# Keys' stacks behind the naturals, gates that begin without GpSimd taps, and rotation tables behind weight halves, in a two-block transformer kernel

## The chip, the cores and the metric

The kernel runs on one core of a Trainium2 chip. The metric is the time of one execution on the device in microseconds (us), given as the median of several runs. The engines are called as the profile calls them: PE is TensorE, ACT is ScalarE, DVE is VectorE, POOL is GpSimd, and SP is SyncE, whose queue issues all the loads here. Line numbers (L113) are those of the kernel before; behind the edits the changed kernel's lines stand up to six lines further down (L113 becomes L114, L488 becomes L489, L521 becomes L524, L908 becomes L914).

## The reference

One sequence of S = 512 tokens and width D = 1024, in float32, passes two blocks. Cut to what matters:

```python
# block 1
h = rms_norm(x, norm1_g)
q, k_c, v_c, k_s, v_s, k_w, v_w, g_nsa, u_conv, g_merge = split(h @ w_in)
# 8 query heads in 2 groups; compressed keys (a 2-layer MLP over windows of 32
# tokens), selected keys and windowed keys; three softmaxes, gated by g_nsa
y_attn = nsa_attention(q, k_c, v_c, k_s, v_s, k_w, v_w, g_nsa, ...) @ w_attn_br
a, gate = split(u_conv)
z = causal_dwconv(a * sigmoid(gate), conv_dw_w) + conv_dw_b      # 31 taps, 512 channels
y_conv = silu(layer_norm(z)) @ w_conv_br
g_a, g_b = split(sigmoid(g_merge))
x = x + (g_a * y_attn + g_b * y_conv) @ w_out
u = causal_dwconv(rms_norm(x) @ ffn_w_up, ffn_dw_w) + ffn_dw_b   # 3 taps
x = rms_norm(x + (silu(u1) * u2) @ ffn_w_down, final_g)
# block 2: two layers, each with a modulation (shift, scale, gate) from c
h = rms_norm(x) * (1 + scale) + shift
x = x + gate * even_mixer(h)   # grouped attention with axial rotations, and a latent attention
x = x + gate * odd_mixer(...)  # windowed attention with a sink per head
return rms_norm(x)
```

The rotation of the even mixer multiplies normalised queries and keys (with a learned gain per head dimension) by cosines and sines. The products of gain and cosine or sine don't depend on the data that flows through the network; they are the "tables" of this change.

## The kernel before

**Products in three parts.** Each float32 weight is split into a high half, rounded for PE, and a low half, the rest. `wload` (L102) does this for a tile of 128 x 512: SP loads the raw tile into a buffer, ACT copies it rounded (L112), and POOL or DVE subtracts (L113). `wpools` says in turn which buffers the next tiles use and which engine subtracts: raw tiles lie in `t` (6 buffers) or `wr` (3), halves in `wh` and `wl` (4 each). A raw buffer is free for the next load when its subtraction is done. `mm3` (L123) makes three products per tile of K, and the first of a group (L133) uses the low half, so that PE waits for the subtraction, and the releaser of such a wait reads "wl L113". A PSUM bank of the pools `pg` and `ps` takes each result and is freed by the evictions that read it.

**Order of the work.** The code is traced top to bottom; then a scheduler lays each engine's instructions out in an order of its own, in which an instruction may overtake others that were traced before it. Two things bind it here: inside `in_order(...)` the named engines keep the traced order, and inside `issue_after(x)` an instruction follows instruction x. Each engine then carries its instructions out strictly in the order laid out; one that waits holds up all that stands behind it on its engine. The same holds for the loads in SP's queue.

**Keys and naturals (L467 to L493).** The two key tiles `tkb` of the selected and the windowed branch are each stacked twice by `stack_k` (L294): two ACT copies (L297, L299) and two DVE operations for each stack, so eight ACT copies in all. Then four "naturals", products with tokens in the partitions, give the values: each is evicted by ACT with a scale (L488), then stacked by `stack_v` (ACT at L305 and DVE), and its gate columns get a tanh (L492). The naturals' PSUM banks are the wide ones, `ps` and `pg` in turn; behind them on PE come the query products and the compression of keys (L425 to L439), whose weights ACT copies at L430, whose sum ACT copies at L436 and PE transposes at L439.

**Merge gates and taps (L685 to L722).** The depthwise convolution's taps are worked beside the sixteen merge gates (`merge_gate(m, b)`, each 24 products with two weight tiles, both subtracted on POOL). Channels 1 to 3 have their taps on DVE, paced by n0 and n1. Channel 0 has its taps on POOL: `conv_tap(0, t)` is a scaled copy on ACT (L520) and an addition on POOL (L521). Those still to be done at this point are in `first`; there are 16 of them, and `gates(0, 7, ...)` spreads them evenly over its 14 gates:

```python
            for t in rest[len(rest) * i // len(todo):len(rest) * (i + 1) // len(todo)]:
                conv_tap(0, t)
```

POOL keeps the traced order here. Ahead of the gates, POOL works at the scores' normalisation (L614) and at the fourth convolution channel's input (L508, L509).

**Down projection and tables (L805 to L911).** The down projection has 22 tiles of K. Tiles 0 to 10 are taken early, tiles 11 to 17 in the loop at L823 over eight column blocks m, whose weight tiles (two per block, one of 128 x 512 and one of 128 x 384) are subtracted on POOL, and tiles 18 to 21 in `by_halves` (L830), first for tokens 0 to 255, then for the rest, so that the normalisation of the first half runs beside the second. The weights of tiles 18 to 21 (`halves_weights`, one tile for each m) stay in the pools `m` and `h`, since both halves use them; they are subtracted on DVE and POOL in turn, and POOL's last, for m = 7, is named `h` in the trace. All of it is independent data, and the scheduler mixes the weight tiles of L823 and of `by_halves`. The four rotation tables are traced behind (L902 to L910), as multiplications on POOL:

```python
            G.tensor_tensor(t, cc(tname).rearrange("p (i d) -> p i d", d=64),
                            row[:, go:go + 64].unsqueeze(1).to_broadcast([128, 4, 64]), op=OP.mult)
```

They need only constants, so the scheduler puts them far ahead of their trace, among the subtractions of L823.

Of the kernel before, what the change touches and what calls it, by code (L numbers as in the profile page):

```python
# [14 lines left out]
OP = mybir.AluOpType  # L15
# [28 lines left out]
def build(ctx, tc, I, out):  # L44
    nc = tc.nc
    PE, A, V, G = nc.tensor, nc.scalar, nc.vector, nc.gpsimd
# [16 lines left out]
    def new(p, shape=(128, 512), dt=F32, tag=None):  # L63
        count[0] += 1
        return pools[p].tile(list(shape), dt, tag=tag or p, name=f"{p}{count[0]}")

    def f(ap):
        return ap.bitcast(F32)
# [4 lines left out]
    row = new("k", (128, 144), tag="row")  # L73
# [4 lines left out]
    def cv(name, i=0, n=1):  # L78
        o = VEC[name][0] + i
        return vec[:, o:o + n]  # L80

    def cc(name, i=0, n=None):
        for t, d in zip(cst, CST):
            if name in d:
                o, m = d[name]
                return t[:, o + i:o + i + (m if n is None else n)]
# [11 lines left out]

    wpools = [[("t", "wh", "wl", G), ("t", "wh", "wl", V), ("wr", "wh", "wl", G)]]
    wcount = [0]  # L100

    def wload(src, kt, n, p=None):  # L102
        wcount[0] += 1
        pr, ph, pl, eng = wpools[0][wcount[0] % len(wpools[0])]
        if p:
            ph, pl = p
        raw = new(pr, (128, 512))
        hi = new(ph, (128, 512), F32R)
        lo = new(pl, (128, 512), F32R)
        z = kt * n  # L110
        nc.sync.dma_start(raw[:, :z], src.rearrange("p k n -> p (k n)"))
        A.activation(hi[:, :z], raw[:, :z], AF.Copy)  # L112
        eng.tensor_sub(lo[:, :z], raw[:, :z], f(hi[:, :z]))  # L113
        return [(hi[:, i * n:(i + 1) * n], lo[:, i * n:(i + 1) * n]) for i in range(kt)]  # L114

    def wsplit(src, kt, n, p=None):
# [177 lines left out]
    def stack_k(src, r0, n=512, dst=None):  # L294
        kh, kl = dst or (new("h", dt=F32R), new("h", dt=F32R))
        o = 64 - r0
        A.activation(kh[r0:r0 + 64, :n], src[r0:r0 + 64, :n], AF.Copy)  # L297
        V.tensor_sub(kl[r0:r0 + 64, :n], src[r0:r0 + 64, :n], f(kh[r0:r0 + 64, :n]))
        A.activation(kh[o:o + 64, :n], src[r0:r0 + 64, :n], AF.Copy)  # L299
        V.tensor_copy(kl[o:o + 64, :n], f(kl[r0:r0 + 64, :n]))  # L300
        return kh, kl
# [55 lines left out]
    with in_order("Activation"):  # L357
        for k in range(KT):
            if k:
                nc.sync.dma_start(X[k], I["xT"][k * 128:(k + 1) * 128, :])  # L360
            hi = new("h", dt=F32R)
            lo = new("h", dt=F32R)
# [22 lines left out]
    for b in range(2):  # L385
        t = new("p")
# [10 lines left out]
    def windows(t, pe):  # L397
        th, tl = split(t, p="p")
        Z = []
        for z in range(2):  # L400
            zh = new("h", (128, 8, 64), F32R)
            zl = new("h", (128, 8, 64), F32R)
            pz = pe[:, 8 * z:8 * z + 8]
            A.activation(zh[:, :, 63], pz, AF.Copy)
            V.tensor_sub(zl[:, :, 63], pz, f(zh[:, :, 63]))
            for zz, ss in ((zh, th), (zl, tl)):
                V.tensor_scalar(zz[:, :, 31], pz, 0.0, None, op0=OP.mult)
                for g in range(2):
                    for o in range(2):
                        dst = zz[64 * o:64 * o + 64, :, g * 32:g * 32 + 31]  # L410
                        src = f(ss[64 * g:64 * g + 64, 16 * o:16 * o + 496]).rearrange("p (n r) -> p r n", r=16)
                        src = src[:, 8 * z:8 * z + 8, :]
                        if zz is zh and o == 0:
                            V.tensor_copy(dst, src)
                        elif zz is zh or g + o == 2:
                            A.activation(dst, src, AF.Copy)
                        else:
                            G.tensor_copy(dst, src)
            Z += [(zh[:, r, :], zl[:, r, :]) for r in range(8)]
        return Z  # L420
# [35 lines left out]
    KB = []  # L456
# [9 lines left out]
    tkb = [new("p") for _ in range(2)]  # L466
# [3 lines left out]
    V.tensor_mul(tkb[1], pkb[1], R1)  # L470
    with after_root():
        ZV = windows(tkv[1], cv("pev", 0, 16))
    for t in tkb:
        KB.append([stack_k(t, 0), stack_k(t, 64)])

    def natural(w, xs, n, i, bank=gemm_bank):
        ps = bank()
# [7 lines left out]
    for i in range(4):  # L485
        ps = natural(wv, xg, 280, i, wide_bank)
        t = new("p")
        A.activation(t[:, 0:280], ps[:, 0:280], AF.Copy, scale=r1[:, i:i + 1])  # L488
        vt = new("h", (128, 4, 128), F32R)  # L489
        stack_v(t[:, 0:256], 4, vt)  # L490
        VB.append(vt)
        A.activation(GN[:, i, :], t[:, 256:280], AF.Tanh, scale=0.5)  # L492
        V.tensor_scalar(GN[:, i, :], GN[:, i, :], 0.5, 0.5, op0=OP.mult, op1=OP.add)  # L493


    zs, conv, attended = [], [], []
# [192 lines left out]
    def gates(m0, m1, n0, n1):  # L689
        todo = [(m, b) for m in range(m0, m1) for b in range(2)]  # L690
        rest = list(first) if m0 == 0 else []
        for i, (m, b) in enumerate(todo):
            if b == 0:
                GM.append([])
            GM[m].append(merge_gate(m, b))
            for c, t in taps[n0 + (n1 - n0) * i // len(todo):n0 + (n1 - n0) * (i + 1) // len(todo)]:
                conv_tap(c, t)
            for t in rest[len(rest) * i // len(todo):len(rest) * (i + 1) // len(todo)]:
                conv_tap(0, t)


# [178 lines left out]
    for th, c in by_halves(I["w_dn"], 18, 22, ACTV[18:], down, "t", ws):  # L880
        v = new("s", (128, 16))[:, 0:4]
        t = new("s", (128, 16))[:, 0:2]
        st = sums[th].st[:, 0:4].rearrange("p (i z) -> p z i", z=2)
        V.tensor_scalar(v[:, 0:2], st[:, 0], 1.0 / D, EPS, op0=OP.mult, op1=OP.add)
        V.tensor_scalar(t, v[:, 0:2], EPS, None, op0=OP.mult)
        V.scalar_tensor_tensor(v[:, 2:4], st[:, 1], 1.0 / D, t, op0=OP.mult, op1=OP.add)
        R = row_bcast(newton(v, sums[th].st), "pt")
        r0 = new("r", tag=("R", "R'")[th])[:, 0:256]
        A.activation(r0, R[:, 0:256], AF.Copy)
        for k in range(KT):  # L890
            modulated(k, fgn[:, k:k + 1], md[:, k:k + 1], R[:, 256:512], c)
        xr.append((r0, c))
        if th == 0:
            wpools[0] = [("t", "wh", "wl", G), ("wr", "wh", "wl", V)]
            wkv = wsplit(I["w_kv"], KT, 256, ("m", "m"))
            wqa = wsplit(I["w_qa"], KT, 512, [("h", "h")] * 2 + [("z", "z")] + [("h", "h")] * 5)
# [6 lines left out]
    for name, go in (("q", 0), ("k", 64)):  # L903
        for tname in ("axc", "axs"):
            if tname == "axc":
                tab = new("b", (128, 2, 4, 64))
            t = tab[:, 0 if tname == "axc" else 1]
            G.tensor_tensor(t, cc(tname).rearrange("p (i d) -> p i d", d=64),  # L908
                            row[:, go:go + 64].unsqueeze(1).to_broadcast([128, 4, 64]), op=OP.mult)
            tabs.append(t)  # L910
    tqc, tqs, tkc, tks = tabs  # L911

# [494 lines left out]
```

## Time and profile before

| | |
|---|---|
| median of 3 runs | 1297.09 us |
| lowest and highest | 1296.65 and 1299.78 us |
| the profiled execution's own time | 1301.25 us |
| its span in the profile | 1299.5 us |
| mean granted clock of PE | 0.989 of full |
| PE busy | 1251.2 us |
| DVE busy | 883.7 us |
| POOL busy | 730.1 us |
| ACT busy | 701.9 us |
| loads | 124.74 MB, mean 96 GB/s |

The rows below come from one profiled execution, and its span is the time from its first to its last recorded instruction. Its own time stands 4.16 us above the median, so a sum of its rows is set against 1301.25 first. A row of the order in time reads: start, duration, engine, line, operation, the tile written and the tiles read with their shapes, the number of instructions (x2), and in brackets the idle time of the engine just before with what ended it. The granted clock is a mean over a stretch: 1.00 is 2.4 GHz, 0.50 is 1.2 GHz.

### The profile page before, as it was taken

The page shows a single profiled execution, that of the slowest core. Times are in us where ns is not written, and L with a number is a line of the kernel's source. Part 1 is how long each engine was busy: PE and PEld are TensorE (multiplying, and loading weights), DVE is VectorE, ACT ScalarE, POOL GpSimd, SP SyncE. Part 2 cuts the span into 40 slices and gives each one's busy share as a digit, 9 for nine tenths or more (in the row PEclk, how much of TensorE's full clock was granted, in tenths as well). Part 3 has the DMA queues.
Part 4 walks back from the last instruction along what each step waited for, and adds up shares of the span by engine and source line. Part 5 has one row for each costly group of instructions (what it writes and reads, how often), then busy time and mean ns, then how long its engine had stood idle before and what let it go on. Part 6 is the DMA issues. An engine that isn't in the chain of part 4 may idle for free. (4 is left out here: it accounts for less than half of the span.)

```text
span 1299.5 us, 19323 instructions
## 1 busy us (share of the span) xinstructions
PE 1251.2 (96%) x6369; PEld 1041.1 (80%) x6369; DVE 883.7 (68%) x2000; ACT 701.9 (54%) x1488; POOL 730.1 (56%) x718
## 2 busy tenths in 40 slices
PE   7999998999999999999999999999999989999997
PEld 6878876888888888888887798877777788888786
DVE  6756666986644878776777258576787766656565
ACT  6756777434444444423443243585766635766554
POOL 5557875773644666655665423386664423676542
PEclk9999998999999999999999999999999989999998
DMA  6221111342434555576553402111111111111221
GB/s 220 90 75 58 33 44 47 91 147 73 138 98 129 165 169 166 161 254 221 171 159 94 145 23 56 49 45 58 53 50 41 33 50 57 58 57 57 66 74 65
DMA packets 71971, 124.74 MB, mean 96 GB/s; under 512 B 8256, under 2 KB 17344, under 8 KB 71872
## 3 DMA queue, kind: packets, MB, share of 16 engines
q1 hardware_dynamic: 71872, 123.52, 30.8%
q8 instruction: 50, 0.82, 0.3%
q14 instruction: 49, 0.40, 0.1%
HBM read 121.39 MB, written 2.10 MB: 95 GB/s over the span
## 5 line engine op out<-in xcount | busy, mean ns | idle before, releaser
L113 POOL TENSOR_TENSOR wl<-wr,wh 128x512 fp32r<-128x512 f32 (+2 forms) x215 | 281.1, 1311 | 260.8 <-ACT wh L112 205.8
L133 PE MATMUL pg<-h,wl 128*128 128x512 f32 x628 | 250.2, 398 | 5.8 <-POOL wl L113 3.9
L135 PE MATMUL pg<-h,wh 128*128 128x512 f32 x628 | 248.0, 395 | 0.0
L134 PE MATMUL pg<-h,wh 128*128 128x512 f32 x628 | 247.6, 394 | 0.0
L112 ACT ACTIVATE wh<-wr 128x512 fp32r<-128x512 f32 (+2 forms) x215 | 132.6, 618 | 164.2 <-PE pg L135 77.7
L133 PEld LDWEIGHTS pg<-h,wl 128*128 128x128 f32 x628 | 119.1, 190 | 29.6 <-POOL wl L113 4.9
L135 PEld LDWEIGHTS pg<-h,wh 128*128 128x128 f32 x628 | 119.0, 189 | 23.3
L134 PEld LDWEIGHTS pg<-h,wh 128*128 128x128 f32 x628 | 119.1, 190 | 22.5 <-issue 0.7
L113 POOL TENSOR_TENSOR m<-t,m 128x512 fp32r<-128x512 f32 (+1 forms) x67 | 89.6, 1337 | 77.3 <-ACT m L112 73.4
L337 DVE TENSOR_TENSOR t<-pt,t 128x512 fp32r<-128x512 f32 (+1 forms) x160 | 97.5, 631 | 28.7 <-ACT t L336 27.4
L342 PE MATMUL po<-t,h 128*128 128x512 f32 (+3 forms) x384 | 110.7, 364 | 4.4 <-DVE t L337 1.9
L133 PE MATMUL ps<-h,wl 128*128 128x512 f32 x260 | 103.1, 396 | 3.2 <-POOL wl L113 3.2
L135 PE MATMUL ps<-h,wh 128*128 128x512 f32 x260 | 102.2, 393 | 0.0
L134 PE MATMUL ps<-h,wh 128*128 128x512 f32 x260 | 101.8, 391 | 0.0
L336 ACT ACTIVATE t<-pt 128x512 fp32r<-128x512 f32 (+1 forms) x160 | 84.3, 552 | 22.6 <-PE pt L332 21.9
L342 PEld LDWEIGHTS po<-t,h 128*128 128x128 f32 x384 | 65.7, 188 | 29.2 <-ACT t L336 13.7
L332 PE MATMUL pt<-k,p 128*128 128x128 f32 x576 | 85.3, 273 | 2.9 <-POOL p L1010 2.9
L332 PEld LDWEIGHTS pt<-k,p 128*128 128x128 f32 x576 | 69.0, 140 | 14.0 <-POOL p L1010 4.4
L1010 POOL TENSOR_SCALAR p<-p,s 128x512 f32<-128x512 f32 x64 | 45.4, 712 | 55.6 <-DVE s L1009 53.5
L778 DVE CUSTOM_DVE_ANT_0 b<-b,z 128x512 f32<-128x512 f32 x48 | 75.5, 1572 | 0.0
L112 ACT ACTIVATE m<-t 128x512 fp32r<-128x512 f32 (+2 forms) x76 | 46.2, 608 | 31.0 <-PE ps L133 9.4
L133 PEld LDWEIGHTS ps<-h,wl 128*128 128x128 f32 x260 | 49.1, 189 | 14.9 <-POOL wl L113 4.8
(441 smaller groups left out, 3046.1 us busy)
## 6 DMA issues: line engine op xcount, KB each, us to landing
b<-ada_t SPq DMA_DIRECT2D x48, 256.0 KB, 3.1
z<-ada_t SPq DMA_DIRECT2D x48, 256.0 KB, 3.2
t<-w_up SPq DMA_DIRECT2D x44, 256.0 KB, 2.9
wr<-w_up SPq DMA_DIRECT2D x44, 256.0 KB, 2.8
wr<-w_g SPq DMA_DIRECT2D x32, 256.0 KB, 2.9
t<-w_dn SPq DMA_DIRECT2D x23, 256.0 KB, 2.7
wr<-w_br SPq DMA_DIRECT2D x16, 256.0 KB, 2.6
wr<-w_gt SPq DMA_DIRECT2D x16, 256.0 KB, 2.9
```

The source lines that it names most:

```text
L112: A.activation(hi[:, :z], raw[:, :z], AF.Copy)
L113: eng.tensor_sub(lo[:, :z], raw[:, :z], f(hi[:, :z]))
L133: PE.matmul(ps, ll, rh, start=start and i == 0, stop=False)
L134: PE.matmul(ps, lh, rl, start=False, stop=False)
L135: PE.matmul(ps, lh, rh, start=False, stop=stop and i == n - 1)
L332: PE.transpose(ps[:, o:o + 128], src, ident)
L336: evac[:] = [A.activation(hi[:, :n], ps[:, :n], AF.Copy)]
L337: evac.append(V.tensor_sub(lo[:, :n], ps[:, :n], f(hi[:, :n])))
L342: PE.matmul(o[:, a:b], v, t[:, pa:pa + b - a], start=start and z == 0, stop=stop and z == 1)
L778: V.tensor_tensor_reduce(out=raw, in0=raw, in1=CA[z], op0=OP.mult, op1=OP.add, scale=1.0, scalar=0.0, accum_out=MA[l][:, z, m:m + 1])
L1010: scaled[0] = G.tensor_scalar(p, p, sm[:, 1:2], 0.0, op0=OP.mult, op1=OP.add)
```

## The change

Three edits move instructions; none adds or removes arithmetic.

1. The keys' stacks are traced inside the loop of naturals: the first key tile's two stacks behind the second natural, the second tile's behind the fourth.
2. In `gates`, channel 0's 16 taps are spread over the third to the fourteenth gate instead of the first to the fourteenth.
3. `wload` keeps the last subtraction that it put on POOL in `halved`. What stands there behind the first half of `by_halves` (the subtraction of the last tile of rows 18 to 21) is kept as `tables_after`, and the four tables are issued after it.

```diff
--- before.py
+++ after.py
@@ -98,6 +98,7 @@
 
     wpools = [[("t", "wh", "wl", G), ("t", "wh", "wl", V), ("wr", "wh", "wl", G)]]
     wcount = [0]
+    halved = []
 
     def wload(src, kt, n, p=None):
         wcount[0] += 1
@@ -110,7 +111,9 @@
         z = kt * n
         nc.sync.dma_start(raw[:, :z], src.rearrange("p k n -> p (k n)"))
         A.activation(hi[:, :z], raw[:, :z], AF.Copy)
-        eng.tensor_sub(lo[:, :z], raw[:, :z], f(hi[:, :z]))
+        sub = eng.tensor_sub(lo[:, :z], raw[:, :z], f(hi[:, :z]))
+        if eng is G:
+            halved[:] = [sub]
         return [(hi[:, i * n:(i + 1) * n], lo[:, i * n:(i + 1) * n]) for i in range(kt)]
 
     def wsplit(src, kt, n, p=None):
@@ -470,8 +473,6 @@
     V.tensor_mul(tkb[1], pkb[1], R1)
     with after_root():
         ZV = windows(tkv[1], cv("pev", 0, 16))
-    for t in tkb:
-        KB.append([stack_k(t, 0), stack_k(t, 64)])
 
     def natural(w, xs, n, i, bank=gemm_bank):
         ps = bank()
@@ -491,6 +492,8 @@
         VB.append(vt)
         A.activation(GN[:, i, :], t[:, 256:280], AF.Tanh, scale=0.5)
         V.tensor_scalar(GN[:, i, :], GN[:, i, :], 0.5, 0.5, op0=OP.mult, op1=OP.add)
+        if i % 2:
+            KB.append([stack_k(tkb[i // 2], 0), stack_k(tkb[i // 2], 64)])
 
 
     zs, conv, attended = [], [], []
@@ -695,7 +698,8 @@
             GM[m].append(merge_gate(m, b))
             for c, t in taps[n0 + (n1 - n0) * i // len(todo):n0 + (n1 - n0) * (i + 1) // len(todo)]:
                 conv_tap(c, t)
-            for t in rest[len(rest) * i // len(todo):len(rest) * (i + 1) // len(todo)]:
+            j, k = max(i - 2, 0), len(todo) - 2
+            for t in rest[len(rest) * j // k:len(rest) * (j + 1) // k] if i > 1 else ():
                 conv_tap(0, t)
 
 
@@ -891,6 +895,7 @@
             modulated(k, fgn[:, k:k + 1], md[:, k:k + 1], R[:, 256:512], c)
         xr.append((r0, c))
         if th == 0:
+            tables_after = halved[0]
             wpools[0] = [("t", "wh", "wl", G), ("wr", "wh", "wl", V)]
             wkv = wsplit(I["w_kv"], KT, 256, ("m", "m"))
             wqa = wsplit(I["w_qa"], KT, 512, [("h", "h")] * 2 + [("z", "z")] + [("h", "h")] * 5)
@@ -905,8 +910,9 @@
             if tname == "axc":
                 tab = new("b", (128, 2, 4, 64))
             t = tab[:, 0 if tname == "axc" else 1]
-            G.tensor_tensor(t, cc(tname).rearrange("p (i d) -> p i d", d=64),
-                            row[:, go:go + 64].unsqueeze(1).to_broadcast([128, 4, 64]), op=OP.mult)
+            with tc.issue_after(getattr(tables_after, "ins", tables_after)):
+                G.tensor_tensor(t, cc(tname).rearrange("p (i d) -> p i d", d=64),
+                                row[:, go:go + 64].unsqueeze(1).to_broadcast([128, 4, 64]), op=OP.mult)
             tabs.append(t)
     tqc, tqs, tkc, tks = tabs
```

PE's order is unchanged. On **ACT**, at the naturals, before (h_494 to h_512 are the keys' stacks, p_547 and p_579 the first two naturals):

```order
L416 ACTIVATE h_481<-p_463 64x8x31
L299 ACTIVATE h_494<-p_426 64x512
L297 ACTIVATE h_500<-p_426 64x512
L299 ACTIVATE h_500<-p_426 64x512
L297 ACTIVATE h_506<-p_427 64x512
L299 ACTIVATE h_506<-p_427 64x512
L297 ACTIVATE h_512<-p_427 64x512
L299 ACTIVATE h_512<-p_427 64x512
L488 ACTIVATE p_547<-ps_522,s_302 128x280
L488 ACTIVATE p_579<-pg_554,s_302 128x280
L305 ACTIVATE h_549<-p_547 128x4x64
L492 ACTIVATE k_521<-p_547 128x24
```

and now (p_523 and p_555 are the same two naturals, h_562 and h_568 the first key tile's stacks):

```order
L419 ACTIVATE h_481<-p_463 64x8x31
L489 ACTIVATE p_523<-ps_498,s_302 128x280
L308 ACTIVATE h_525<-p_523 128x4x64
L493 ACTIVATE k_497<-p_523 128x24
L489 ACTIVATE p_555<-pg_530,s_302 128x280
L308 ACTIVATE h_557<-p_555 128x4x64
L493 ACTIVATE k_497<-p_555 128x24
L300 ACTIVATE h_562<-p_426 64x512
L302 ACTIVATE h_562<-p_426 64x512
L300 ACTIVATE h_568<-p_426 64x512
L302 ACTIVATE h_568<-p_426 64x512
```

The two naturals' evictions stand ahead of all eight stack copies; the second key tile's four come behind the fourth natural.

On **POOL**, around the second of the first gate's two weight tiles (wl_2766) and, further down, at the second gate (wl_2808, wl_2814; h_1077 is channel 0's sum), before:

```order
L521 TENSOR_TENSOR h_1077<-h_1077,r_2094 128x512
L113 TENSOR_TENSOR wl_2766<-wr_2764,wh_2765 128x512
L508 TENSOR_SCALAR p_2173<-p_2173 128x512
L509 TENSOR_TENSOR z_2176<-p_2134,p_2173 128x512
L614 TENSOR_SCALAR p_2182<-p_2182,s_2189,k_521 128x128
L614 TENSOR_SCALAR p_2183<-p_2183,s_2198,k_521 128x256
```

```order
L521 TENSOR_TENSOR h_1077<-h_1077,r_2661 128x512
L521 TENSOR_TENSOR h_1077<-h_1077,t_2803 128x512
L113 TENSOR_TENSOR wl_2808<-wr_2806,wh_2807 128x512
L113 TENSOR_TENSOR wl_2814<-wr_2812,wh_2813 128x512
L521 TENSOR_TENSOR h_1077<-h_1077,t_2851 128x512
L113 TENSOR_TENSOR wl_2856<-wr_2854,wh_2855 128x512
```

and now (the second gate's tiles are wl_2805 and wl_2811, the third's wl_2850 and wl_2856):

```order
L114 TENSOR_TENSOR wl_2766<-wr_2764,wh_2765 128x512
L114 TENSOR_TENSOR wl_2805<-wr_2803,wh_2804 128x512
L114 TENSOR_TENSOR wl_2811<-wr_2809,wh_2810 128x512
L511 TENSOR_SCALAR p_2173<-p_2173 128x512
L512 TENSOR_TENSOR z_2176<-p_2134,p_2173 128x512
```

```order
L524 TENSOR_TENSOR h_1077<-h_1077,r_2661 128x512
L114 TENSOR_TENSOR wl_2850<-wr_2848,wh_2849 128x512
L114 TENSOR_TENSOR wl_2856<-wr_2854,wh_2855 128x512
L524 TENSOR_TENSOR h_1077<-h_1077,t_2894 128x512
L114 TENSOR_TENSOR wl_2899<-wr_2897,wh_2898 128x512
L114 TENSOR_TENSOR wl_2905<-wr_2903,wh_2904 128x512
```

The second gate's two subtractions stand behind the first gate's, ahead of the convolution input, and the first tap of the gates comes behind the third gate's subtractions. In SP's queue the two loads of the second gate's weights stand correspondingly earlier.

On **POOL**, at the tables (b_8038, b_8041), in the down projection, before:

```order
L113 TENSOR_TENSOR wl_7207<-wr_7205,wh_7206 128x384
L799 TENSOR_TENSOR p_7036<-p_7036,p_7081 128x512
L908 TENSOR_TENSOR b_8038<-k_8036,k_108 128x256 x2
L113 TENSOR_TENSOR wl_7236<-t_7234,wh_7235 128x512
L113 TENSOR_TENSOR wl_7242<-wr_7240,wh_7241 128x384
L799 TENSOR_TENSOR p_7138<-p_7138,p_7183 128x512
L113 TENSOR_TENSOR wl_7271<-t_7269,wh_7270 128x512
L908 TENSOR_TENSOR b_8041<-k_8036,k_108 128x256 x2
L113 TENSOR_TENSOR wl_7277<-wr_7275,wh_7276 128x384
```

and now (h_7665 is the last tile of rows 18 to 21, for m = 7; wl_7376 and wl_7382 belong to the sixth column block of L823):

```order
L114 TENSOR_TENSOR wl_7341<-t_7339,wh_7340 128x512
L114 TENSOR_TENSOR h_7617<-t_7615,h_7616 128x512
L114 TENSOR_TENSOR wl_7347<-wr_7345,wh_7346 128x384
L114 TENSOR_TENSOR h_7665<-t_7663,h_7664 128x512
L914 TENSOR_TENSOR b_8038<-k_8036,k_108 128x256 x2
L914 TENSOR_TENSOR b_8041<-k_8036,k_108 128x256
L114 TENSOR_TENSOR wl_7376<-t_7374,wh_7375 128x512
L914 TENSOR_TENSOR b_8041<-k_8036,k_108 128x256
L114 TENSOR_TENSOR wl_7382<-wr_7380,wh_7381 128x384
L114 TENSOR_TENSOR wl_7411<-t_7409,wh_7410 128x512
```

Three tables now stand in a row between the last tile of rows 18 to 21 and the sixth column block's first subtraction, the fourth between that block's two; none is left at the old places.

## Rows read from the trace of the kernel before

**Rows 1.** The page's busy table: busy us, share of the span, instructions.

```profile
PE 1251.2 (96%) x6369; PEld 1041.1 (80%) x6369; DVE 883.7 (68%) x2000; ACT 701.9 (54%) x1488; POOL 730.1 (56%) x718
```

**Rows 2.** Who waits for whom, PE alone: us in total, times, longest us.

```profile
PE pg L133 <- POOL wl L113: 3.9, 2, 3.7
...
PE pg L133 <- ACT p L488: 1.9, 1, 1.9
```

**Rows 3.** Table of stretches: us, PE busy (products), granted clock, DMA share, GB/s.

```profile
49.00:55.00 6.00, 5.43 (x17) 0.72 0.01 3
217.00:227.00 10.00, 8.96 (x27) 0.66 0.40 113
725.40:735.40 10.00, 9.84 (x42) 1.00 0.58 180
240.00:260.00 20.00, 20.00 (x90) 1.00 0.34 93
```

**Rows 4.** Order in time, ACT, at the naturals.

```profile
41.52 2.47 ACT L416 ACTIVATE h<-p 64x248 fp32r<-64x248 f32 x4 [0.57 <-DVE p L162]
...
47.89 0.63 ACT L299 ACTIVATE h<-p 64x512 fp32r<-64x512 f32 x1
...
48.93 0.49 ACT L488 ACTIVATE p<-pg,s 128x280 f32<-128x280 f32 x1
```

**Rows 5.** Order in time, PE, behind the second natural's eviction and at the compressed keys.

```profile
49.56 0.48 PE L133 MATMUL pg<-h,wl 128*128 128x512 f32 x1 [1.88 <-ACT p L488]
...
61.06 0.66 PE L439 MATMUL pg<-k,p 64*128 64x64 f32 x4 [0.57 <-ACT p L436]
```

**Rows 6.** Order in time, ACT, ahead of the compressed keys.

```profile
57.36 0.63 ACT L112 ACTIVATE wh<-t 128x512 fp32r<-128x512 f32 x1
...
60.65 0.36 ACT L436 ACTIVATE p<-pg 64x256 f32<-64x256 f32 x1
```

**Rows 7.** Order in time, POOL, at the fourth convolution input and the second gate.

```profile
173.89 0.62 POOL L508 TENSOR_SCALAR p<-p 128x512 f32<-128x512 f32 x1 [4.91 <-ACT p L505]
...
215.10 1.66 POOL L521 TENSOR_TENSOR h<-h,t 128x512 f32<-128x512 f32 x1 [10.62 <-ACT t L520]
216.72 2.52 POOL L113 TENSOR_TENSOR wl<-wr,wh 128x512 fp32r<-128x512 f32 x2
```

**Rows 8.** Order in time, PE, at the second gate.

```profile
218.04 0.80 PE L133 MATMUL pg<-h,wl 128*128 128x512 f32 x1 [3.74 <-POOL wl L113]
```

**Rows 9.** Order in time, ACT, beside the first pair of tables.

```profile
695.98 0.61 ACT L112 ACTIVATE wh<-t 128x512 fp32r<-128x512 f32 x1
```

**Rows 10.** Order in time, POOL: tables at two places, the first also alone, and the sixth block.

```profile
696.05 1.89 POOL L908 TENSOR_TENSOR b<-k,k 128x256 f32<-128x256 f32 x2 [0.63 <-DVE p L789]
697.89 1.30 POOL L113 TENSOR_TENSOR wl<-t,wh 128x512 fp32r<-128x512 f32 x1
...
696.05 0.74 POOL L908 TENSOR_TENSOR b<-k,k 128x256 f32<-128x256 f32 x1 [0.63 <-DVE p L789]
...
709.68 2.33 POOL L908 TENSOR_TENSOR b<-k,k 128x256 f32<-128x256 f32 x2
...
725.20 1.29 POOL L113 TENSOR_TENSOR h<-t,h 128x512 fp32r<-128x512 f32 x1
726.44 1.29 POOL L113 TENSOR_TENSOR wl<-t,wh 128x512 fp32r<-128x512 f32 x1
```

**Rows 11.** Order in time, PE, in the down projection.

```profile
709.77 0.50 PE L133 MATMUL ps<-h,wl 128*128 128x512 f32 x1 [0.80 <-POOL wl L113]
...
725.29 0.50 PE L133 MATMUL ps<-h,wl 128*128 128x512 f32 x1 [1.53 <-POOL wl L113]
...
727.79 0.50 PE L133 MATMUL pg<-h,wl 128*128 128x512 f32 x1 [0.16 <-POOL wl L113]
```

**Rows 12.** Table of stretches, DVE: us, DVE busy (instructions), granted clock, DMA share, GB/s.

```profile
696.05:696.79 0.74, 0.68 (x1) 1.00 0.00 0
709.68:712.01 2.33, 2.33 (x4) 1.00 0.50 140
725.50:729.00 3.50, 0.00 (x0) 1.00 0.76 217
```

## The prediction

> **What bounds the kernel now.** I read the page's busy table first: TensorE (PE) is busy 1251.2 of 1299.5 us [rows 1]. With every other engine at 68% or less, only the 48.3 us in which PE is idle, or time in which it runs at a lower clock, can be won or lost. Next came the list of who waits for whom, for PE alone. Two kinds of wait in it belong to the places that the diff touches: a product that waits for ScalarE's (ACT's) copy at line 488, once, 1.9 us, and products that wait for GpSimd's (POOL's) weight subtraction at line 113, 3.9 us in two waits, of which one is 3.7 [rows 2]. Third, the table of stretches, for the granted clock. The 6 us around 52 us ran at a mean of 0.72 of the full clock and the 10 us around 222 us at 0.66, and both stretches begin at a long wait of PE; the 10 us behind 725.4 us ran at 1.00 [rows 3]. The level below full is the half (1.2 instead of 2.4 GHz), so these stretches lost 6 x 0.28 = 1.7 us and 10 x 0.34 = 3.4 us beside the waits themselves. Last came the order in time, engine by engine, at the three places.
>
> **Part 1, keys' stacks behind the naturals.** It removes nothing and adds nothing: eight ACT copies (lines 297, 299) and eight operations of VectorE (DVE) move behind evictions. Now the stacks' copies run on ACT, 0.63 us each (47.89 is the last), and only then come the two evictions of line 488 that free PSUM banks [rows 4]. The next product needs the bank of the second one, and starts at 49.56, after 1.88 us idle [rows 5]. In the new order two evictions stand ahead of all stacks. Six copies of line 416 still precede (the last four start at 41.52 and take 2.47, to 44.0, less 0.6 for a stack that ran ahead of them); the first natural's three ACT operations take about 1.1 us and the second eviction 0.49, so the bank is free near 45.0, before PE asks at 47.7. Gain: 1.9 us of wait, and with it the 1.7 us at the half clock.
>
> Not all of 3.6 us survives. Four stacks (4 x 0.63 = 2.5 us) now stand behind the fourth natural, so ACT is busy to about 52.5, where it idled before. PE would end the query product 3.6 us earlier; from there ACT runs a chain of its own, from the weight copy at 57.36 to the end of the copy of the compressed keys, 61.01 (60.65 plus 0.36) [rows 6], 3.65 us, and PE waits for that copy, 0.57 us now [rows 5]. Ahead of the chain stand weight copies of the compression, the last of which needs the end of the query product; now it starts with it, in the new order about 0.4 us behind it, since the copies ahead of it come late. So ACT reaches the chain's end 3.2 us earlier, not 3.6, and PE waits 0.4 us more there. I take **-3.2 us**. Ends: -1.9 (wait only, the clock as it was) and -3.6.
>
> **Part 2, the first two gates without GpSimd taps.** Now POOL's order at the gates is tap, then two subtractions for the second gate's weights. The tap (line 521) waits for ACT's scaled copy until 215.10, after 10.62 us of idle, takes 1.66, and the two subtractions take 2.52 more [rows 7]. PE waits for the first of them: 3.74 us idle until 218.04 [rows 8], and the clock falls to half behind it [rows 3]. In the new order the two subtractions stand behind the first gate's, ahead of the fourth convolution input. Their place is the idle of 4.91 us that ends at 173.89 [rows 7], since the ACT halves are made there already. 2 x 1.26 us go into it [rows 7]; the second may overlap its end, by 0.5 us at most, on work that the scores need two steps later. They free two load buffers, so two loads of gate weights are issued some 45 us earlier; nothing queued behind them on the load queue is needed before the gates. So the wait goes, 3.7 us, and the slow stretch, 3.4 us: **-7.1 us**. Ends: -3.7 (the clock falls anyway) and -7.4.
>
> What covers the moved taps: 16 taps on 14 gates become 16 on 12. PE does 90 products in 20 us at the gates [rows 3], 0.222 us each, so a gate's 24 products are 5.3 us; POOL has two subtractions and one or two taps for it, at 1.26 us each [rows 7] at most 5.0. PE sees none of it as long as that holds.
>
> **Part 3, the rotation tables.** Four multiplications move on POOL. Now one pair runs at 696.05 (1.89 us) and one at 709.68 (2.33 us) [rows 10]. In the new order they stand behind the subtraction of the down projection's last weight half, which runs at 725.20: three at once, then the subtraction for the sixth column block (now at 726.44), then the fourth. Two effects. First, the gain at the old places. The subtraction behind the first pair had its ACT half by 696.6 [rows 9] and started at 697.89, 1.3 us late; it frees a load buffer, and the loads, ACT halves and subtractions of the next 30 us hang on one another through these buffers. I give 1.0 of the 1.3 us to that chain, since DVE works beside the subtraction at its new time and can slow it. PE's wait at 709.77, 0.80 us, goes; that at 725.29 stays as long as it is, 1.0 us earlier [rows 11]. Second, the cost at the new place. The last half's subtraction ends at 725.5 instead of 726.5; three tables at 0.74 us (the first of the four by itself) make 2.2; the subtraction that PE waits for ends at 729.0 instead of 727.7. PE loses **1.3 us**, and stands idle some 2.7 us before it, from 726.3 (725.29 less 1.0, and nine products) to 729.0. Now the idle there is 0.16 us.
>
> Beside the wait stands the clock. In this trace a wait of 1.88 us was followed by the half clock [rows 3, 5], one of 1.53 us, at 725.29, by 1.00 [rows 3, 11]. 2.7 us is past the first, so I add **1.7 us**, the smaller of the two prices. What is queued behind the tables: loads of the next stage's weights, issued 1 to 2 us later. The program multiplies by them only behind the down projection's last half and the normalisation, so that hides.
>
> The price of a table has two ends: 0.74 us, and 1.17 us (half of 2.33). In the 2.33 us of the dearer pair DVE worked all the time, on four instructions; in the 3.5 us behind 725.5 it ran none [rows 12], so I take the lower. The Trainium skill (GPSIMD Engine Reference, section 1, Specifications) says that GpSimd's memory interfaces are shared with VectorE, with contention for DVE instructions with two operands in SBUF; an idle DVE would then mean the lower price, as taken, and the sum at the end would stay -7.3. By the higher price it would be -6.0. The trace does not decide it alone, since DVE was busy for 0.68 of the 0.74 us of the cheaper table too [rows 12].
>
> **Sum.** -3.2 - 7.1 + 1.3 + 1.7 = -7.3 us. The profiled execution, whose rows these are, took 1301.25 us with a span of 1299.5, so 1293.95 against its own time. It is 4.2 us above the median of the runs, 1297.09; against that median the forecast is **1289.8 us**.
>
> **Rivals.**
> - *The clock gives nothing.* The half-clock stretches do not hang on the waits and come back elsewhere. For it: the profiled run is 4.2 us above the median, so such stretches may differ from run to run. Against it: both stand right behind a wait here. -1.9 - 3.7 + 1.3 = -4.3, 1292.8 us.
> - *The tables cost more.* 1.17 us each: 3 x 0.43 = 1.3 us more, and the long slow stretch (3.4 us, as at 218) instead of the short one: -7.3 + 1.3 + 1.7 = -4.3, also 1292.8 us.
> - *The tables cost nothing.* The front of the chain moves up by more than I give it, or the last half's subtraction meets idle time, and PE is not held: -3.2 - 7.1 = -10.3, 1286.8 us.
> - *Taps crowd out subtractions, slower.* Four of the twelve gates now carry two taps, four POOL operations in 5.3 us. At 1.26 us they fit; from 1.33 us each they do not. The tap at 215.10 took 1.66 [rows 7], and DVE has taps of its own all through the gates: 4 x 1.66 = 6.6, 1.3 us of wait at each of four gates, with 1.7 us of half clock each, 12.0 us: -7.3 + 12.0 = +4.7, 1301.8 us. Against it: the two subtractions behind that tap ran at 1.26 [rows 7].
> - *It does not do what it says.* The words are that the tables queue behind the last weight halves; the program's order puts them ahead of subtractions that PE still waits for, which is what part 3 costs. For the other parts: another wait, hidden now, ends just as late (DVE's evictions at the gates are the nearest), and the gain is under 3.9 us.
>
> **Numbers.** Forecast 0.57; clock gives nothing 0.13; tables cost more 0.11; tables cost nothing 0.09; crowded 0.04; other wait 0.06. A measurement of this kernel tells 0.3% from no change, 3.9 us: the bound for faster is 1293.2. The forecast and the free tables lie wholly under it (0.66), the two cases at 1292.8 for some 0.6 of their 0.24 (0.14): faster 0.80, same 0.16, slower 0.04. For the range, the free tables and the full gains give 1286 at best, the two dearer cases with a miss of 1.5 us on top 1294.5: 1285.5 to 1294.5.
>
> **What would show it.** Part 1: the product now at 49.56 starts without idle and the clock stays at 1.00 near 50 us; the copy of line 436 comes about 3 us earlier. Part 2: no wait at the second gate, clock 1.00 there, two subtractions in the idle near 173 us. Part 3: three tables in a row on POOL, an idle of PE of 2 to 3 us behind them, half clock after it. A wait of PE on POOL inside the later gates, or a slow stretch without a wait ahead of it, would prove the account wrong.

## The result, and the profile after

The changed kernel takes **1288.6 us** (median of 5 runs, 1288.21 to 1291.48). The kernel before, in the 5 runs beside it, takes 1299.09 us (1296.65 to 1301.12; the median of 1297.09 that the forecast starts from was that of the first three). The ratio is 0.993, with a 95% interval of 0.9915 to 0.9945, so some 9 us less. The forecast was 1289.8 us, in a range of 1285.5 to 1294.5.

The page's busy table of the changed kernel, against [rows 1]:

```profile
PE 1244.2 (97%) x6369; PEld 1036.3 (81%) x6369; DVE 883.1 (69%) x2000; ACT 700.3 (54%) x1488; POOL 728.3 (57%) x718
```

DVE, ACT and POOL are busy as long as before, within 2 us. PE is busy 7.0 us less with as many instructions, at a mean granted clock of 0.995 instead of 0.989, and idle 5.9 us less (42.4 against 48.3). These are two single executions, and some of the difference lies where no edit reaches: 1.1 us of the idle ahead of the program's first product (5.2 against 6.3 us), and 1.6 and 1.5 us of the clock around 312 and 1060 us of the kernel before.

The list of who waits for whom, PE alone, of the changed kernel, against [rows 2] (line numbers are up to six higher now):

```profile
PE pg L136 <- POOL wl L114: 2.2, 1, 2.2
...
PE ps L136 <- POOL wl L114: 1.6, 2, 1.2
```

The wait for ACT's copy (1.9 us) and that for the second gate's subtraction (3.7 us) are gone. One wait of 2.2 us is new. The table of stretches of the changed kernel for PE, against [rows 3], behind the sixth block's first product, at the second and third gates, and at the query product:

```profile
715.06:721.06 6.00, 6.00 (x19) 0.72 0.45 131
210.00:220.00 10.00, 10.00 (x46) 1.00 0.31 106
47.00:53.00 6.00, 6.00 (x32) 1.00 0.00 0
```

Two slow stretches are gone, and one has come, behind the new wait. Next the order in time, ACT, of the changed kernel, against [rows 4, 6]:

```profile
43.59 0.47 ACT L489 ACTIVATE p<-pg,s 128x280 f32<-128x280 f32 x1
...
44.54 0.62 ACT L300 ACTIVATE h<-p 64x512 fp32r<-64x512 f32 x1
...
50.98 0.63 ACT L302 ACTIVATE h<-p 64x512 fp32r<-64x512 f32 x1
...
56.16 0.36 ACT L439 ACTIVATE p<-pg 64x256 f32<-64x256 f32 x1
```

The second natural is evicted by 44.06, ahead of all stacks, whose last copy ends at 51.6; the copy of the compressed keys starts 4.49 us earlier than before, of which 0.83 us were gained ahead of the naturals, where no edit is. And PE, against [rows 5, 11]:

```profile
46.69 0.39 PE L136 MATMUL pg<-h,wl 128*128 128x512 f32 x1
...
56.57 0.66 PE L442 MATMUL pg<-k,p 64*128 64x64 f32 x4 [0.62 <-ACT p L439]
...
706.35 0.50 PE L136 MATMUL ps<-h,wl 128*128 128x512 f32 x1 [0.44 <-POOL wl L114]
...
710.53 0.50 PE L136 MATMUL ps<-h,wl 128*128 128x512 f32 x1 [1.16 <-POOL wl L114]
...
715.06 0.50 PE L136 MATMUL pg<-h,wl 128*128 128x512 f32 x1 [2.18 <-POOL wl L114]
```

The query product starts without idle. In the down projection the first wait is gone and the sixth block's is 2.18 instead of 0.16. On POOL, against [rows 7, 10]:

```profile
168.81 1.28 POOL L114 TENSOR_TENSOR wl<-wr,wh 128x512 fp32r<-128x512 f32 x1 [1.43 <-ACT wh L113]
170.06 0.62 POOL L511 TENSOR_SCALAR p<-p 128x512 f32<-128x512 f32 x1
...
210.56 3.11 POOL L114 TENSOR_TENSOR wl<-wr,wh 128x512 fp32r<-128x512 f32 x2 [10.47 <-ACT wh L113]
213.64 1.29 POOL L524 TENSOR_TENSOR h<-h,t 128x512 f32<-128x512 f32 x1
...
711.69 2.10 POOL L914 TENSOR_TENSOR b<-k,k 128x256 f32<-128x256 f32 x3
713.75 1.26 POOL L114 TENSOR_TENSOR wl<-t,wh 128x512 fp32r<-128x512 f32 x1
```

The second gate's last subtraction ends as the convolution input begins (170.06). POOL's idle of 10.5 us at the gates now ends with the third gate's subtractions, and the first tap comes behind them. Three tables take 2.10 us ahead of the subtraction that the sixth block waits for.

**Where the time went, by place.** PE's order is the same in both kernels, so the time between the starts of the same two products can be compared in any two traces. The table gives it (us) for stretches that run, in the kernel before, from 47.0 to 62.0 (query product), 212.5 to 230.0 (second and third gate), 690.0 to 739.9 (down projection), and for two in which nothing was changed. The rows below the second are the change's second profile and the experiments.

| kernel | query | gates | down | 298.9 to 318.1 | 759.3 to 785.1 |
|---|---|---|---|---|---|
| before | 14.97 | 17.47 | 49.95 | 19.21 | 25.80 |
| the change | 11.31 | 10.69 | 51.76 | 17.64 | 25.80 |
| the change, again | 11.29 | 10.66 | 50.24 | 17.63 | 25.81 |
| part 1 alone | 11.26 | 17.16 | 49.57 | 19.21 | 30.45 |
| part 2 alone | 13.02 | 10.69 | 49.79 | 17.63 | 30.45 |
| part 3 alone | 15.24 | 17.60 | 51.82 | 19.21 | 25.79 |
| parts 1 and 2 | 11.29 | 10.69 | 49.69 | 19.22 | 25.81 |
| tables last | 11.26 | 10.69 | 48.30 | 19.22 | 25.81 |
| one table there | 11.26 | 10.69 | 48.83 | 19.22 | 25.83 |
| two tables there | 11.26 | 10.66 | 49.65 | 19.20 | 30.44 |
| tables last, halves on DVE | 11.26 | 10.69 | 47.04 | 17.63 | 30.44 |
| taps from the second gate | 11.26 | 10.69 | 51.85 | 17.63 | 25.80 |
| taps on 8 gates | 11.84 | 10.69 | 49.99 | 17.64 | 25.80 |
| taps on 5 gates | 11.71 | 10.69 | 50.10 | 19.22 | 25.81 |

Part 1 gives 3.7 us, part 2 gives 6.8, part 3 takes between 0.3 and 1.9 against the kernel before. The last two columns are either of two values, though no edit reaches into these stretches. A profile is one execution, so they are not a property of the kernel in whose row they stand.

### The profile page after: what moved, and what is told of

Its sections match the earlier page's. It is cut to its first block, busy times and chain, and to the rows that moved or that the text cites. A ratio compares the mean times of both kernels' runs of the same rounds, so it can differ in the third digit from the quotient of the medians.

```text
span 1286.6 us, 19323 instructions
## 1 busy us (share of the span) xinstructions
PE 1244.2 (97%) x6369; PEld 1036.3 (81%) x6369; DVE 883.1 (69%) x2000; ACT 700.3 (54%) x1488; POOL 728.3 (57%) x718
```

## The experiments

**Each part alone, and two together.** Theory A: each part works at its own place, by the wait and by the half clock behind it. B: the half clock hangs on no place and comes back elsewhere, so that only the waits are won. C: the parts need each other. From the change, parts are undone; part 3 as here, part 2 by the old bounds of `rest`, part 1 by the old place of `KB.append`:

```diff
-            with tc.issue_after(getattr(tables_after, "ins", tables_after)):
-                G.tensor_tensor(t, cc(tname).rearrange("p (i d) -> p i d", d=64),
-                                row[:, go:go + 64].unsqueeze(1).to_broadcast([128, 4, 64]), op=OP.mult)
+            G.tensor_tensor(t, cc(tname).rearrange("p (i d) -> p i d", d=64),
+                            row[:, go:go + 64].unsqueeze(1).to_broadcast([128, 4, 64]), op=OP.mult)
```

Part 1 alone:

> Only the keys' stacks move; gates and tables as before. Theory A (each part acts at its own place, and the half-clock stretch behind a removed wait goes with the wait): 3.7 us less than before (2.1 of wait, 1.6 of clock), PE without idle at the query product and clock 1.00 there; the second gate's wait of 3.7 us and its slow stretch are still there. Theory B (the half-clock stretches come back elsewhere): 2.1 us less, with a new slow stretch in the trace. Theory C (the parts need each other: what part 1 wins is lost again at the second gate's wait): within 1 us of before, that wait longer by 2 to 4 us.

Measured 1295.64 against 1298.3 us, ratio 0.9977 (0.9961 to 0.9992): faster by 3.0 us, with an interval of 1.0 to 5.1 that holds both A's 3.7 and B's 2.1. At the place it is 11.26 against 14.97 us, 3.7 less, as A has it. The second gate's wait is as long as before, so C falls. The order in time, PE, of part 1 alone at the second gate:

```profile
214.36 0.79 PE L136 MATMUL pg<-h,wl 128*128 128x512 f32 x1 [3.75 <-POOL wl L114]
```

And its table of stretches, PE, at the query product and in a stretch far from any edit:

```profile
49.00:55.00 6.00, 6.00 (x38) 1.00 0.05 17
770.00:775.00 5.00, 5.00 (x25) 0.50 0.29 82
```

There was a new slow stretch, as B says, in a place where part 2 alone and two kernels with parts 1 and 2 have it too (30.4 us in the last column). This run alone doesn't decide between A and B.

Part 2 alone:

> Only the first two gates lose their GpSimd taps; stacks and tables as before. Theory A: 6.6 us less than before (3.8 of wait, 2.8 of clock). Theory B: 3.8 us less. In both the wait of 1.9 us at the query product and the half clock behind it are still there.

Measured 1293.63 us, ratio 0.9967 (0.9954 to 0.9979): 4.3 us less, with an interval of 2.7 to 6.0 that leaves A's 6.6 out and holds B's 3.8. At the place it is 10.69 against 17.47, 6.8 less, as A has it. So the runs show less than the place. The profiled execution took 30.45 us in the last column instead of 25.80; whether that stretch is slow more often with part 2 alone stays open. The wait at the query product was there, but shorter, and no half clock came behind it. Order in time and table of stretches, PE, of part 2 alone:

```profile
49.38 0.47 PE L136 MATMUL pg<-h,wl 128*128 128x512 f32 x1 [1.53 <-ACT p L491]
```

```profile
49.00:55.00 6.00, 5.62 (x25) 1.00 0.08 24
```

Part 3 alone:

> Only the tables move; stacks and gates as before. Theory A: 1.5 us more than before: the front gains 1.8, the wait for the sixth block's first weight half rises to about 2.2 us and costs 1.7, and 1.6 us of half clock follow. Theory B: no difference within 0.5 us. By the forecast's own terms it would be 3.0 us more (front 1.0, wait 1.3 net, clock 1.7). A rival in which the tables cost nothing there: 1.8 us less than before.

Measured 1300.76 us, ratio 1.001 (0.9993 to 1.0027): between 0.9 us less and 3.5 more, which takes in A (1.5), the forecast's own terms (3.0) and B (no difference), and leaves out free tables (1.8 less). At the place 51.82 against 49.95, 1.9 more. Order in time and table of stretches, PE, of part 3 alone:

```profile
727.45 0.50 PE L136 MATMUL pg<-h,wl 128*128 128x512 f32 x1 [2.20 <-POOL wl L114]
```

```profile
727.45:733.45 6.00, 6.00 (x19) 0.72 0.42 132
```

Parts 1 and 2:

> The change without its third part: stacks and gates changed, tables as before. Theory A: 10.3 us less than before, so about 1.5 us less than the change as a whole; waits of 0.8 and 0.3 us in front and 1.5 us ahead of the sixth block, clock 1.00 there. Theory B: 5.9 us less than before, the same as the change as a whole. Rival (tables cost nothing at their new place): 1.8 us more than the change as a whole.

Measured 1289.73 us, ratio 0.9928 (0.9909 to 0.9947): 9.3 us less, interval 6.9 to 11.8. B's 5.9 falls out. Against the change as a whole (0.993) no difference can be told by the runs. By place it is 49.69 against 51.76 and 50.24: part 3 costs 0.5 to 2.1 us.

**The clock over all runs.** Every run has its mean granted clock on record, not only the profiled one. The 29 runs of the kernel before that stand beside these four experiments go from 1295.07 us at a clock of 0.994 to 1305.01 us at 0.986, so they differ mainly by the clock. The span times one minus the clock estimates what the half clock cost a run. The mean clock is 0.9917 in the kernel before, 0.9917 with part 1 alone, 0.9922 with part 2 alone, 0.9894 with part 3 alone and 0.9935 with parts 1 and 2. For parts 1 and 2 together that is 2.4 us less (1.2 to 3.6), which is more than B's nothing and less than A's 4.4. With part 1 or part 2 alone the gain is not seen: 0.7 us less for part 2 (between 1.9 less and 0.6 more), none for part 1 (1.6 either way). Part 3 alone has 3.0 us more (1.0 to 4.9), where A has 1.6. So A holds for the waits, and for the half clock at the places in the profiles; in the mean of the runs only about half of the clock's gain is there. Whether the rest comes back elsewhere, or the kernel before doesn't lose it in every run, is not shown.

**How many tables ahead of the sixth block.** All, three, two, one or none of them stand where the change puts them; the others come behind the last subtraction of rows 11 to 17, where POOL is idle. With none:

```diff
         V.tensor_add(X[m], X[m], ps)
+    last_down = halved[0]
...
-            tables_after = halved[0]
+            tables_after = last_down
```

> The change with all four tables behind the last subtraction of rows 11 to 17, where GpSimd has nothing to do. Theory A (the wait at the sixth block is that of the three tables, 3 x 0.73 us, and the half clock follows the wait): the wait of 2.2 us falls to at most 0.2, clock 1.00 behind it, 3.4 us less than the change as a whole. Theory B (the clock follows no place): 1.8 us less. Rival (the sixth block waits for something else that is as late, its ACT half or its load): no difference, the wait stays near 2 us with another releaser.

Measured 1288.45 us, ratio 0.9919 (0.9907 to 0.9931). Order in time, PE, of this kernel:

```profile
713.89 0.50 PE L136 MATMUL ps<-h,wl 128*128 128x512 f32 x1 [1.10 <-POOL wl L114]
...
716.39 0.50 PE L136 MATMUL pg<-h,wl 128*128 128x512 f32 x1 [0.17 <-POOL wl L114]
```

The wait is 0.17, so it was that of the tables, and the stretch takes 48.30 us: 1.4 less than with the tables at their old places, 1.9 to 3.5 less than with the change. The change again, on the same chip:

> The change as a whole once more, beside the others on one chip. All theories: about 9 us less than before, a wait of 2.2 us at the sixth block, half clock behind it.

Measured 1289.54 us, ratio 0.9935 (0.9921 to 0.9948). Order in time and table of stretches, PE, of this second profile of the changed kernel:

```profile
715.32 0.50 PE L136 MATMUL pg<-h,wl 128*128 128x512 f32 x1 [2.21 <-POOL wl L114]
```

```profile
715.32:721.32 6.00, 6.00 (x26) 1.00 0.43 132
```

The wait came as expected; the half clock did not. The same kernel, at the same wait, once at 0.72 and once at 1.00.

> The change with one table ahead of the sixth block's subtractions and three behind the last one of rows 11 to 17. Theory A: a wait of 0.7 to 0.9 us there, no half clock behind it (a wait of 1.53 us had none), 2.6 to 2.8 us less than the change as a whole. Theory B: 1.4 us less.

> The change with two tables ahead of the sixth block's subtractions and two behind the last one of rows 11 to 17. Theory A: a wait of 1.4 to 1.6 us there; the rows so far have a wait of 1.53 us without a half clock and one of 1.88 with it, so the clock most likely stays at 1.00: 2.4 us less than the change as a whole, 0.7 if it falls. Theory B: 0.7 us less in either case.

Measured 1288.08 us (0.9921, 0.9908 to 0.9934) and 1289.83 us (0.9932, 0.9918 to 0.9946). Order in time, PE, with one table and with two:

```profile
715.72 0.50 PE L136 MATMUL pg<-h,wl 128*128 128x512 f32 x1 [0.83 <-POOL wl L114]
```

```profile
716.44 0.50 PE L136 MATMUL pg<-h,wl 128*128 128x512 f32 x1 [1.50 <-POOL wl L114]
```

The wait follows the number of tables: 0.17, 0.83, 1.50 and 2.18 to 2.21 us for none, one, two and three, 0.68 us each. Clock 1.00 followed the first three; the table of stretches, PE, with two tables:

```profile
716.44:722.44 6.00, 6.00 (x26) 1.00 0.45 142
```

The whole times of these kernels lie within each other's intervals; a gain of 2 us is below what the runs tell.

**Room for the taps.** The bounds 2 and 14 of the change become 1 and 14, 2 and 10, 2 and 7; here 2 and 10:

```diff
-            j, k = max(i - 2, 0), len(todo) - 2
-            for t in rest[len(rest) * j // k:len(rest) * (j + 1) // k] if i > 1 else ():
+            j, k = max(i - 2, 0), 10 - 2
+            for t in rest[len(rest) * j // k:len(rest) * (j + 1) // k] if 2 <= i < 10 else ():
```

> The change with the 16 taps over 13 gates, from the second on. Theory A (only the second gate's subtractions had no time to wait for a tap): the scaled copy comes near 211 us as in the change, the tap ends near 213, the third gate's first subtraction near 214.3, and PE asks for it at 215.2: no wait, the gates' 17 us take 10.7 as in the change. Rival (the third gate needs its subtractions ahead of taps too): a wait of 1 to 3 us at the third gate.

One run, 1289.71 us. POOL's order in time at the third gate:

```profile
211.26 1.68 POOL L524 TENSOR_TENSOR h<-h,t 128x512 f32<-128x512 f32 x1 [10.62 <-ACT t L523]
212.90 2.55 POOL L114 TENSOR_TENSOR wl<-wr,wh 128x512 fp32r<-128x512 f32 x2
```

No wait of PE at the gates, and 10.69 us there: sparing one gate would have done.

> The change with the 16 taps over 8 gates, two for each. By the forecast's terms POOL has 2 x 1.28 + 2.55 = 5.1 us of work for 5.46 us of products: no wait of PE on POOL at the gates. The forecast's slower rival (taps crowd out subtractions, 1.66 us a tap): 0.4 us and more of wait at each of eight gates.

One run, 1290.98 us. PE and POOL in the order in time:

```profile
238.10 0.50 PE L136 MATMUL ps<-h,wl 128*128 128x512 f32 x1 [0.35 <-POOL wl L114]
...
244.61 0.50 PE L136 MATMUL pg<-h,wl 128*128 128x512 f32 x1 [0.78 <-POOL wl L114]
```

```profile
232.74 2.66 POOL L524 TENSOR_TENSOR h<-h,t 128x512 f32<-128x512 f32 x2
236.76 2.54 POOL L114 TENSOR_TENSOR wl<-wr,wh 128x512 fp32r<-128x512 f32 x2 [1.36 <-ACT wh L113]
239.24 2.68 POOL L524 TENSOR_TENSOR h<-h,t 128x512 f32<-128x512 f32 x2
```

A miss: 1.1 us of wait, in two places. A tap takes 1.33 us here and the four operations 5.2, less than a gate's 5.44, but POOL idles 1.36 us in between for ACT's halves, so that its round, from 232.74 to 239.24, is 6.5 us.

> The change with the 16 taps over 5 gates, three for each and four for the last. 3 x 1.28 + 2.55 = 6.4 us of POOL's work for 5.46 us of products, 0.9 us too much at each gate and 2.2 at the last, 6 us in all, less a lead of about 3 us that POOL has at the third gate: 2 to 4 us of waits on POOL, the first of them behind the fourth crowded gate at the earliest. If POOL's lead is larger than that, no wait.

One run, 1297.54 us, about as slow as before. PE in the order in time:

```profile
233.74 0.50 PE L136 MATMUL pg<-h,wl 128*128 128x512 f32 x1 [0.99 <-POOL wl L114]
...
240.37 0.50 PE L136 MATMUL ps<-h,wl 128*128 128x512 f32 x1 [0.87 <-POOL wl L114]
...
248.18 0.79 PE L136 MATMUL pg<-h,wl 128*128 128x512 f32 x1 [2.08 <-POOL wl L114]
```

3.9 us of waits, as expected, the first one gate earlier than I had put it, and a slow stretch behind the last: between the same two products, from 230.0 to 259.9 before, lie 36.35 us instead of 29.92. The forecast's rival in which taps crowd out subtractions is a real mechanism; the change's spread over 12 gates stays clear of it.

**A further step: the other subtractions off GpSimd.** From the kernel with the tables last:

```diff
-                    ws.append(halves_weights(src, k0, k1, raw, m))
+                    ws.append(halves_weights(src, k0, k1, raw, m, engines=(V, V) if src is I["w_dn"] else (G, V)))
```

> As the kernel with all tables behind the last subtraction of rows 11 to 17, and GpSimd's three subtractions of rows 18 to 21 given to VectorE, which idles there for 3 to 8 us at a time. Theory A (the waits left there, 0.35, 0.36, 1.10 and 0.17 us, come from GpSimd working at these subtractions while PE wants the others): the 1.10 falls to 0.2 or less, the stretch of 50 us around it is 0.9 to 1.3 us shorter. Rival (ScalarE's halves or the loads are what comes late): the waits stay within 0.2 us of what they were.

Measured 1289.16 us, ratio 0.9936 (0.992 to 0.9953). Order in time, PE:

```profile
705.96 0.50 PE L136 MATMUL ps<-h,wl 128*128 128x512 f32 x1 [0.34 <-POOL wl L114]
...
711.67 0.50 PE L136 MATMUL pg<-h,wl 128*128 128x512 f32 x1 [0.64 <-POOL wl L114]
```

The 1.10 is gone, the sixth block's wait rose from 0.17 to 0.64, and the stretch is 1.3 us shorter (47.04), 3.2 to 4.7 less than with the change. The runs don't show it: the median is not below that of the tables last alone. The profiled execution had the slow 30.44 us in the last column. By place this is the best version; by whole times no version is shown to beat the change.

## Why the prediction was right

**Part 1** was put at -3.2 and gave -3.7. The mechanism held: two evictions ahead of the stacks, the wait gone, the half clock behind it gone. The 0.4 us that I had given back to ACT's later chain were not due: PE's wait for the compressed keys is 0.62 us, against 0.57 [rows 5]. So the step "PE waits 0.4 us more there" was wrong.

**Part 2** was put at -7.1 and gave -6.8 at its place, in every kernel that has it: 10.66 to 10.69 us against 17.16 to 17.60 in the three that have not. The cover held too: the taps on 12 gates delay nothing. The price of the half clock was 0.4 us too high. The 10 us from 217.00 [rows 3] hold 1.0 us of the wait itself, which the forecast had counted as wait already. From the wait's end the kernel before ran at 0.70, so 3.0 us were lost and not 3.4:

```profile
218.04:228.04 10.00, 9.99 (x32) 0.70 0.45 133
```

**Part 3** was put at +3.0 and costs +0.3 in one profile of the change and +1.8 in the other. The loss by the wait, net of the gain in front, was put at 1.3 us and is 0.2 to 0.3, because the front of the chain moved up by 1.8 us where I had allowed 1.0 (by the starts of the same products, 1.5 us up to that at 713.04 and the rest by 725.29). The idle of PE was foreseen at 2.7 us and is 2.2. Most of this is a misreading: I let PE reach the wait at 726.3, nine products of 0.222 us behind its start, but by [rows 11] these nine take 2.34 us (725.29 to 727.79, less 0.16 idle). The price for a table, 0.74 us with DVE idle, held: 2.10 us for three, 0.73 for the fourth. DVE's table of stretches of the changed kernel, during the three tables:

```profile
711.69:713.79 2.10, 0.00 (x0) 1.00 0.81 226
```

The Trainium skill (GPSIMD Engine Reference, section 1, Specifications) has GpSimd share its memory interfaces with VectorE; the trace agrees in so far as DVE, idle there, left the tables at the lower of the two prices.

The other step that was off is "2.7 us is past the first, so I add 1.7 us". It took the clock behind a wait as certain. Behind the sixth block's wait with three tables ahead the clock fell in three profiles (2.18, 2.20 and 2.20 us) and stayed at 1.00 in three (2.21, 2.63 and 2.65 us, the last two in the kernels with crowded taps, eight gates and five):

```profile
717.58 0.50 PE L136 MATMUL pg<-h,wl 128*128 128x512 f32 x1 [2.63 <-POOL wl L114]
717.58:723.58 6.00, 6.00 (x26) 1.00 0.40 131
```

```profile
724.07 0.50 PE L136 MATMUL pg<-h,wl 128*128 128x512 f32 x1 [2.65 <-POOL wl L114]
724.07:730.07 6.00, 6.00 (x26) 1.00 0.43 131
```

When the clock falls there, it costs 1.6 us, near the 1.7 of the forecast. The Trainium skill (TensorE: Matmul & The Clock Gate, Part 1) says of the rise at a kernel's start that its place varies from run to run for one and the same kernel. The two profiles of the change show the like at a fall: 0.72 and 1.00 behind the same wait.

Together the places give between -10.2 and -8.6 us, the runs -10.5 by the medians and -9.1 by the ratio. Two misses of mine, 0.5 in part 1 and 1.2 to 2.7 in part 3, both went the same way, and so the change came out larger than the forecast's 7.3. That the time lies only 1.2 us below the forecast is in part luck: the forecast counts from 1297.09 us, the median of three runs, and the same kernel took 1299.09 beside the change and 1298.25 in the median of the 51 runs beside the experiments. From 1299.09 the forecast would have been 1291.8 us, 3.2 above the measured time.

Of the forecast's rivals, free tables are out by part 3 alone, and dearer tables by their 2.10 us. "The clock gives nothing" is out for parts 1 and 2 together, by the clock of the runs (2.4 us, 1.2 to 3.6), but the forecast's full price of the clock, 5.1 us for parts 1 and 2, is out too. The sign I had set for an account gone wrong, a slow stretch without a wait ahead of it, does occur, in four kernels of this study (30.4 us in the last column) and not at the edits: the account holds for the three places and not for all of the clock.

## What to carry to other kernels

Work that an engine could do later is not free ahead of work that PE waits for, even when the engine is idle half of the time: look at what stands in front of each subtraction or eviction in its engine's order, and what that waits for. A wait of 2 to 4 us on PE can cost about twice its length, since half clock may follow; one of 1.5 us or less had none at the places edited here. Where effects are below the spread of the runs, compare the time between the same two instructions in several traces.

## What was not expected of the hardware

- The half clock behind a wait is not sure. At waits of 3.74 and 3.75 us it came in three of three profiles, at 1.88 and 2.11 (query product) in two of two, at 2.08 (three taps on a gate) in one of one, at 2.18 to 2.65 (sixth block) in three of six, at 1.53 and less in none of the edited places.
- The length of a wait alone doesn't decide it. In block 2, where no edit reaches, PE waits 2.02 or 2.03 us for DVE in all fourteen profiles, and the clock fell behind it in five. The two profiles of the change, first the one and then the other:

```profile
1048.28 0.39 PE L136 MATMUL ps<-h,h 128*128 128x256 f32 x1 [2.02 <-DVE x L1162]
1048.28:1054.28 6.00, 6.00 (x50) 1.00 0.02 4
```

```profile
1046.89 0.39 PE L136 MATMUL ps<-h,h 128*128 128x256 f32 x1 [2.03 <-DVE x L1162]
1046.89:1052.89 6.00, 6.00 (x37) 0.72 0.00 0
```

- It also comes with hardly a wait at all. The stretch from 759.3 to 785.1 took 25.8 us in ten of the fourteen profiles and 30.4 in four, with no wait of PE in it or in the 19 us ahead of it above 0.3 us, and no edit reaches into it. That from 298.9 to 318.1 took 19.2 us in eight and 17.6 in six, with no wait in it above 0.5 us. Part 1 alone ran at 0.50 from 770 to 775 us; the kernel before:

```profile
770.00:775.00 5.00, 4.74 (x42) 1.00 0.18 48
```

- What decides it in such a stretch was not found.
- A round of work on POOL is not the sum of its instructions: with two taps on a gate 1.36 us of idle for ACT's halves belong to it, and a sum of 5.2 us was too slow for a gate of 5.44.
